# An encoder layer pair on one core: from a scheduler's order to an order fixed by the program

## The chip, the cores and the metric

One core of a Trainium2 chip. The metric is the device time of the whole program in microseconds (us). All arithmetic is float32 in and out; products run on TensorE either as true float32 or as float32r, a faster format into which a float32 number is split in two parts (high and low).

## The reference

Two sequences (2048 and 512 tokens, width 1024) pass through one even and one odd layer with the same weights. Cut to what matters:

```python
# even layer
u = x @ w_in                                  # q,k,v,z of GLA; decay input; q,k,v,z of banded attention
ya = gla_mixer(qa, ka, va, za, gd, ...)       # gated linear attention, forward and backward in time
yb = swa_mixer(qb, kb, vb, zb, rel_bias, sink)# |i-j| <= 128, 8 heads, 2 key/value heads
x = layer_norm(alpha * x + concat([ya, yb]) @ w_out)
# odd layer
bg, cg, h, z = split(x @ w_in, 4)
conv = conv3(cg * h)                          # over time, width 3, per channel
x = layer_norm(alpha * x + (silu(z) * bg * conv) @ w_out)
```

## The kernel before, in words

The 2560 tokens are five groups of 512 (groups 0 to 3 are the long sequence, 4 the short one) and 20 chunks of 128. Intermediate results go through DRAM tensors (`q_s`, `k_s`, `d_s`, `mix_s`, `x1_s` and so on). The work falls into stages.

- **Dense stages.** `e1(g)` projects a group: eight weight tiles moving (`dense_tok`, L207) and 21 blocks with the weights stationary (`dense_ch`, L193). `out_even(g)` is the output projection with residual and layer norm, `odd(g)` the odd layer: 32 blocks (eight times z, c, h, b) and an output projection. Every dense product is three float32r passes: weight high times input high and low (L200, L201), weight low times input high (L204). `weight` (L177) loads a weight tile `ws`, casts it to `wh` on ScalarE, and subtracts on GpSimd to get `wl`; three `ws` and two each of `wh` and `wl` exist.
- **Attention.** `bwd` (L415) runs over the chunks from the last to the first and stores a state for each. `gla` (L450) does one chunk: seven levels of doubling block size, each with DVE products of keys and queries with decays (L520, L525, L527) and a set of small matmuls (L474, L505, L511, L514), then the products with the values and the states (L545, L554). `swa` (L580) does one banded block: scores (L605, L606), bias and maximum (L607), exponential (L616), scaling (L620), transposes (L627), copies (L630, L632) and the value product in true float32 (L635).
- **Order.** The Tile scheduler sets the order on each engine from priorities: matmuls of dense stages in the order of the program text, all that goes through `Urgent` (L97) ahead of the rest; so an instruction of a dense stage's other engines goes first, and attention fills in as the scheduler's own model of time finds it ready. In `run` (L809) `e2_group(g)` is chunk by chunk `gla` and then `swa`; `odd(4)` and `out_even(0)` come after all groups.
- Instructions that go through `Urgent` are all put down to L108; they are told apart by their tiles.

Of the kernel before, what the change touches and what calls it, by code (L numbers as in the profile page):

```python
# [10 lines left out]
F32 = mybir.dt.float32  # L11
# [6 lines left out]
D = 1024  # L18
# [12 lines left out]
def make_layout(i):  # L31
    """Host side: slices, transposes and replicas of the inputs, and arrays that depend on shapes alone."""
# [64 lines left out]
class Urgent:  # L97
    """An engine whose instructions are scheduled ahead of those that are not urgent."""

    def __init__(self, tc, engine):  # L100
        self.tc, self.engine = tc, engine

    def __getattr__(self, name):
        f = getattr(self.engine, name)

        def call(*a, **k):
            with self.tc.high_priority(1000000):
                return f(*a, **k)  # L108
        return call


class Engines:
    def __init__(self, tc, nc, tensor):
        self.tensor = Urgent(tc, nc.tensor) if tensor else nc.tensor
        self.vector, self.scalar, self.gpsimd, self.sync = (
            Urgent(tc, e) for e in (nc.vector, nc.scalar, nc.gpsimd, nc.sync))


class Trunk:
    def __init__(self, tc, nc, I, y_out, ctx):  # L120
        self.tc, self.nc, self.I, self.y_out = tc, nc, I, y_out
        self.dense = Engines(tc, nc, False)
        self.first = Engines(tc, nc, True)
# [6 lines left out]
        self.md = P("mdp", 4)  # L130
        self.mg = P("mgp", 3)
        self.ms = P("msp", 3)
        self.small = P("small", 3)
# [10 lines left out]
        self.qb_s = dr("qb_s", (NC, 64, 8, 128))  # L144
        self.kb_s = dr("kb_s", (64, 2, T))
        self.vb_s = dr("vb_s", (NC, 128, 128))
# [3 lines left out]
        self.up = None  # L150
        self.mix_s = dr("mix_s", (NG, 2, 128, 4, 512))
        self.x1_s = dr("x1_s", (T, D))
        self.sf = {}

    # ---------------------------------------------------------------- helpers
# [12 lines left out]
    def mG(self, shape=(128, 512), dt=F32):  # L168
        return self.mg.tile(list(shape), dt, tag="mg", name="mg")

    def mS(self, shape=(128, 512), dt=F32):
        return self.ms.tile(list(shape), dt, tag="ms", name="ms")
# [4 lines left out]
    def weight(self, src, n=1024):  # L177
        """Load n columns of float32 weights and split them exactly into two float32r parts."""
        nc = self.dense
        raw = self.wp.tile([128, 1024], F32, tag="ws", name="ws", bufs=3)[:, :n]  # L180
        nc.sync.dma_start(raw, src)
        hi = self.wp.tile([128, 1024], F32R, tag="wh", name="wh")[:, :n]
        lo = self.wp.tile([128, 1024], F32R, tag="wl", name="wl")[:, :n]
        nc.scalar.copy(hi, raw)
        nc.gpsimd.tensor_tensor(lo, raw, hi.bitcast(F32), op=ALU.subtract)
        return hi, lo

    def split(self, raw, hi, lo):
        nc = self.dense
        nc.scalar.copy(hi, raw)  # L190
        nc.vector.tensor_tensor(lo, raw, hi.bitcast(F32), op=ALU.subtract)

    def dense_ch(self, src, xh, xl):  # L193
        """[128 channels, 512 tokens] = w^T x, weights stationary."""
        nc = self.dense
        wh, wl = self.weight(src.rearrange("p k c -> p (k c)"))
        p = self.acc.tile([128, 512], F32, tag="acc", name="acc")
        for k in range(8):
            c = slice(k * 128, k * 128 + 128)
            nc.tensor.matmul(p[:], wh[:, c], xh(k), start=(k == 0), stop=False)  # L200
            nc.tensor.matmul(p[:], wh[:, c], xl(k), start=False, stop=False)  # L201
        for k in range(8):
            c = slice(k * 128, k * 128 + 128)
            nc.tensor.matmul(p[:], wl[:, c], xh(k), start=False, stop=(k == 7))  # L204
        return p

    def dense_tok(self, src, n, tiles):  # L207
        """[128 tokens, n columns] per token tile, weights moving. tiles: list of (xh(k), xl(k), pool)."""
        nc = self.dense
        out = []  # L210
        for i, t in enumerate(tiles):
            out.append(self.acc.tile([128, 512], F32, tag="acc", name="acc")[:, :n] if i < 4 else self.pw()[:, :n])
        for kc in range(4):
            wh, wl = self.weight(src[kc].rearrange("p k c -> p (k c)"), 2 * n)
# [11 lines left out]
            for (xh, xl), p in zip(tiles, out):  # L226
                high(xh, xl, p)
                if kc == 3:
                    low(xh, p)
            if kc < 3:  # L230
                for (xh, xl), p in zip(tiles, out):
                    low(xh, p)
        return out

    def log_sig(self, z, out):
        """out = log(sigmoid(z)) = min(z, 0) - log(1 + exp(-|z|))"""
        nc = self.dense
# [5 lines left out]
    def silu(self, z, out, g=None):  # L243
        """out = silu(z) (times g per partition)"""
        nc = self.dense
# [7 lines left out]
    def rstd(self, nc, out, var, scale, eps):  # L253
        nc.scalar.activation(out, var, AF.Ln, scale=scale, bias=eps)
        nc.scalar.activation(out, out, AF.Exp, scale=-0.5)

    # ---------------------------------------------------------------- constants
    def load(self, n, shape, dt=F32):
        t = self.const.tile(list(shape), dt, name=n)
        self.dense.sync.dma_start(t[:], self.I[n])  # L260
        return t

    def setup(self):
        nc, I, c = self.nc, self.I, self.const
# [11 lines left out]
    def setup_up(self):  # L276
        """The up-projections of the decays, split into float32r parts and stacked, with the bias as two rows."""
        nc, I = self.dense, self.I
        self.up = []
        raw = self.e2.tile([128, 4, 512], F32, tag="QK", name="QK")  # L280
        hi = self.e2.tile([128, 2, 512], F32R, tag="Q", name="Q")
        for d, n in enumerate("bf"):
            nc.sync.dma_start(raw[:, d], I["up_" + n])
            lo = raw[:, 2 + d]
# [3 lines left out]
            st = self.e2.tile([128, 512], F32R, tag="ln" + n, name="ln" + n)  # L288
            nc.vector.scalar_tensor_tensor(st[:], hi[:, d].bitcast(F32), self.hl[:, 0:1], lo, op0=ALU.mult, op1=ALU.add)
            self.up.append(st)  # L290

    def setup_late(self):
        nc, I, c = self.nc, self.I, self.const
# [8 lines left out]
    def setup_bias(self):  # L302
        nc, I, c = self.nc, self.I, self.const
        oh = self.mS((32, 512))
        nc.sync.dma_start(oh[:], I["onehot"])
        ml = self.mS((8, 512))
        nc.sync.dma_start(ml[:], I["mline"])
        rb = c.tile([32, 8], F32, name="relb")
        nc.sync.dma_start(rb[:], I["relb"])
        p = self.pw()  # L310
        nc.tensor.matmul(p[:8], rb[:], oh[:], start=True, stop=True)
        line = self.mS((8, 512))
        nc.vector.tensor_tensor(line[:], p[:8], ml[:], op=ALU.add)
        nc.sync.dma_start(self.line_s, line[:])
        for h in range(8):
            rows = self.mS()
            nc.sync.dma_start(rows[:], self.line_s[h:h + 1].broadcast_to([128, 512]))
            nc.sync.dma_start(self.bias_s[h], rows[:])
        self.bias = c.tile([128, 8, 384], F32, name="bias")
        b = self.bias_s  # L320
        nc.sync.dma_start(self.bias[:], bass.AP(b.tensor, b.offset + 127, [[511, 128], [65536, 8], [1, 384]]))

    # ---------------------------------------------------------------- even layer, projections
    def e1(self, g):
        nc, I = self.dense, self.I
        xh, xl = [], []
        for hf in range(2):
            lo = self.stp.tile([128, 4, 512], F32R, tag="st", name="st")
            hi = self.stp.tile([128, 4, 512], F32R, tag="st", name="st")
            for k in range(0, 4, 2):  # L330
                n = 1 if g in (0, 4) else 2
                if g:
                    r = self.yp.tile([128, 2, 512], F32, tag="y", name="y")
                    r = [r[:, 0:1], r[:, 1:2]] if n == 1 else [r[:]]
                else:
                    r = [self.m2((128, 1, 512))[:] for _ in range(2)]
                for i, t in enumerate(r):
                    nc.sync.dma_start(t, I["xT"][g, hf, :, k + i:k + i + n])
                    for j in range(n):
                        self.split(t[:, j], hi[:, k + i + j], lo[:, k + i + j])  # L340
            xh.append(hi)
            xl.append(lo)
        fh = lambda k: xh[k // 4][:, k % 4]
        fl = lambda k: xl[k // 4][:, k % 4]
# [3 lines left out]
        p0 = self.dense_tok(I["w_tok"][0], 336, tiles)  # L348
        for t in range(4):
            v = self.m2()  # L350
            nc.scalar.copy(v[:, :336], p0[t])
            nc.sync.dma_start(self.v_s[4 * g + t, :, :336], v[:, :336])
        p1 = self.dense_tok(I["w_tok"][1], 336, tiles)
        rs = []
        for t in range(4):
            r = self.m2()
            nc.vector.tensor_copy(r[:, :336], p1[t])
            nc.sync.dma_start(self.v_s[4 * g + t, :, 336:], r[:, :176])
            nc.sync.dma_start(self.vb_s[4 * g + t], r[:, 176:304])
            rs.append(r)  # L360
        pg = self.pd()
        for t in range(4):
            nc.tensor.transpose(pg[:32, t * 128:t * 128 + 128], rs[t][:, 304:336], self.ident[:])
        if self.up is None:
            self.setup_up()
        G = self.m2(dt=F32R)
# [489 lines left out]
```

## Time and profile before

| | us |
|---|---|
| median of 3 runs (lowest, highest) | 2750.6 (2750.18, 2762.8) |
| span of the profiled execution | 2753.3 |
| TensorE busy in it (share) | 2582.3 (94%) |
| VectorE (DVE) busy | 1488.7 (54%) |
| ScalarE (ACT) busy | 1201.6 (44%) |
| GpSimd (POOL) busy | 929.6 (34%) |
| DMA: share of the 16 engines, all queues | 49.4% |

The span runs from the first to the last instruction of the profiled execution; no other time of that execution is given. A matmul's row shows how long one takes from start to end; they overlap, so the pace is read from one start to the next. In rows of a timeline the columns are start, length, engine, line, operation, tiles (written<-read), count, and in brackets the idle time ahead with what ended it. In rows of stretches they are the stretch, its length, the busy time of each engine with its instructions, and then the granted clock of TensorE and the DMA's share.

### The profile page before, as it was taken

The numbers are of one execution on the slowest core, as the hardware profiler recorded it, in microseconds if no ns is written. First come the engines' busy times: TensorE is split into PE (matmuls) and PEld (weight loads), VectorE is DVE, ScalarE is ACT, GpSimd is POOL, SyncE is SP. The second block draws the span as 40 slices with busy tenths as digits, with TensorE's granted clock in tenths as the row PEclk, the third lists the DMA queues.
The fourth block names the chain that finished last, engine by engine and source line by source line (L and its number), as shares of the span: only waits on it lengthen the run. The fifth ranks groups of instructions, "written<-read, shape, count | busy, mean of one in ns | idle before, by whom it ended". The sixth has DMA issues, their size and how long they took to land.

```text
span 2753.3 us, 41852 instructions
## 1 busy us (share of the span) xinstructions
PE 2582.3 (94%) x16214; PEld 2034.7 (74%) x16214; DVE 1488.7 (54%) x2595; ACT 1201.6 (44%) x2246; POOL 929.6 (34%) x409
## 2 busy tenths in 40 slices
PE   8999999899999989999988889989999999999998
PEld 7887876687778866666665666668788878878887
DVE  3222377632252277787778877863553455345335
ACT  5545555345435545444443344443334423432431
POOL 3433322233434412212222222224444434434442
PEclk9999999999999999999999999999999999999999
DMA  7667554557458644343445464423652355234322
GB/s 251 192 204 227 157 168 138 171 178 220 148 169 263 187 144 124 101 139 110 142 131 189 153 196 134 126 77 103 209 176 93 134 176 180 92 123 156 112 96 88
DMA packets 258549, 425.19 MB, mean 154 GB/s; under 512 B 38656, under 2 KB 152064, under 8 KB 258352
## 3 DMA queue, kind: packets, MB, share of 16 engines
q1 hardware_dynamic: 258352, 422.53, 49.0%
q8 instruction: 128, 2.10, 0.3%
q14 instruction: 69, 0.57, 0.1%
HBM read 339.59 MB, written 82.85 MB: 153 GB/s over the span
## 4 chain that ended last, share of the span: by engine, by line
PE 39%; DVE 6%; issue 2%; DMA 2%; ACT 1%; SPq 0%; DVEq 0%; ACTq 0%
PE acc L201 8%; PE acc L200 8%; PE acc L204 8%; PE acc L224 3%; PE acc L220 3%; PE acc L219 3%; PE pss L635 1%; DVE y L108 1%; PE pss L627 1%; PE psg L545 1%; DMA md<-mix_s 1%; DVE QK L525 1%; DMA md<-x_s 1%; DMA P<-kb_s 0%; PE psg L474 0%
## 5 line engine op out<-in xcount | busy, mean ns | idle before, releaser
L108 POOL TENSOR_TENSOR wl<-ws,wh 128x1024 fp32r<-128x1024 f32 (+1 forms) x381 | 902.3, 2369 | 1679.4 <-PE acc L204 829.4
L200 PE MATMUL acc<-st,wh 128*128 128x512 f32 x2120 | 844.0, 398 | 0.0
L201 PE MATMUL acc<-st,wh 128*128 128x512 f32 x2120 | 842.7, 397 | 0.0
L108 ACT CAST wh<-ws 128x1024 fp32r<-128x1024 f32 (+1 forms) x381 | 388.0, 1018 | 586.3 <-PE acc L201 214.6
L204 PE MATMUL acc<-st,wl 128*128 128x512 f32 x2120 | 547.2, 395 | 0.0
L200 PEld LDWEIGHTS acc<-st,wh 128*128 128x128 f32 x2120 | 404.1, 191 | 81.8 <-issue 2.6
L201 PEld LDWEIGHTS acc<-st,wh 128*128 128x128 f32 x2120 | 404.1, 191 | 80.2 <-issue 0.4
L204 PEld LDWEIGHTS acc<-st,wl 128*128 128x128 f32 x2120 | 396.0, 188 | 82.5 <-issue 3.0
L219 PE MATMUL acc<-wh,st 128*128 128x512 f32 (+1 forms) x872 | 324.4, 375 | 20.2 <-ACT st L108 13.3
L220 PE MATMUL acc<-wh,st 128*128 128x512 f32 (+1 forms) x872 | 322.3, 372 | 0.0
L108 ACT ACTIVATE md<-md 128x512 f32<-128x512 f32 x360 | 227.6, 632 | 123.4 <-DVE md L108 116.1
L108 DVE SCALAR_TENSOR_TENSOR md<-acc,md 128x512 f32<-128x512 f32 x120 | 82.7, 689 | 357.8 <-ACT md L108 354.9
L224 PE MATMUL acc<-wl,st 128*128 128x512 f32 (+1 forms) x872 | 220.3, 371 | 0.0
L219 PEld LDWEIGHTS acc<-wh,st 128*128 128x128 f32 x872 | 167.1, 192 | 47.0 <-ACT st L108 13.7
L220 PEld LDWEIGHTS acc<-wh,st 128*128 128x128 f32 x872 | 167.3, 192 | 21.5 <-DVE st L108 0.2
L224 PEld LDWEIGHTS acc<-wl,st 128*128 128x128 f32 x872 | 157.0, 191 | 24.2 <-issue 3.4
L108 ACT ACTIVATE md<-acc 128x512 f32<-128x512 f32 x160 | 93.7, 597 | 73.5 <-PE acc L204 67.7
L635 PE MATMUL pss<-ms,V 128*64 128x512 f32 x224 | 119.4, 622 | 6.2 <-DVE ms L632 6.0
L108 DVE TENSOR_TENSOR md<-md,acc 128x512 f32<-128x512 f32 x40 | 27.5, 687 | 179.8 <-PE acc L204 179.8
L108 ACT CAST st<-md 128x512 fp32r<-128x512 f32 x88 | 53.5, 620 | 159.1 <-DVE md L108 131.3
L627 PEld LDWEIGHTS pss<-ident,P 128*128 128x128 f32 x448 | 56.5, 145 | 88.7 <-DVE P L620 44.5
L627 PE MATMUL pss<-ident,P 128*128 128x128 f32 x448 | 92.2, 292 | 31.4 <-DVE P L620 31.4
(170 smaller groups left out, 2987.1 us busy)
## 6 DMA issues: line engine op xcount, KB each, us to landing
ws<-in_w_od SPq DMA_DIRECT2D x160, 512.0 KB, 3.5
ws<-in_w_ch SPq DMA_DIRECT2D x105, 512.0 KB, 3.7
ws<-in_w_oe SPq DMA_DIRECT2D x40, 512.0 KB, 3.6
ws<-in_w_oo SPq DMA_DIRECT2D x40, 512.0 KB, 3.5
ws<-in_w_tok SPq DMA_DIRECT2D x40, 336.0 KB, 2.9
d_s<-md SPq DMA_DIRECT2D x40, 256.0 KB, 3.1
tA<-d_s SPq DMA_DIRECT2D x20, 512.0 KB, 4.6
P<-qb_s SPq DMA_DIRECT2D x40, 256.0 KB, 4.6
```

Source lines behind the costliest of these rows:

```text
L108: return f(*a, **k)
L200: nc.tensor.matmul(p[:], wh[:, c], xh(k), start=(k == 0), stop=False)
L201: nc.tensor.matmul(p[:], wh[:, c], xl(k), start=False, stop=False)
L204: nc.tensor.matmul(p[:], wl[:, c], xh(k), start=False, stop=(k == 7))
L219: nc.tensor.matmul(p, xh(k), wh[:, c], start=(k == 0), stop=False)
L220: nc.tensor.matmul(p, xl(k), wh[:, c], start=False, stop=False)
L224: nc.tensor.matmul(p, xh(k), wl[:, c], start=False, stop=(k == 7))
L525: nc.vector.tensor_tensor(qq, qq, tot(1, n - 1), op=ALU.mult)
L545: nc.tensor.matmul(po[:, h], l, r, start=(i == 0), stop=(i == len(mm) - 1))
L627: nc.tensor.transpose(pt[:, gq], Pt[:, 4 * kv + gq, kb * 128:kb * 128 + 128], self.ident[:])
L635: nc.tensor.matmul(po[64 * kv:64 * kv + 64], V[:, kb, 64 * kv:64 * kv + 64], PT[kv][:], start=(kb == 0), stop=(kb == nk - 1), tile_positio ...
```

## The change

The scheduler is switched off (`manual_schedule`), and the program text is the order of each engine. The text is produced by a small planner, `Flow`: dense stages are one generator, all else is "side" generators. A generator yields after each piece with numbers of its own: TensorE time, a wait until its next piece may follow, and DVE time. The planner adds these up in a clock of its own and, at each yield of the dense generator (in a weight-stationary block: after 8 matmuls, after 16, and behind its evacuation), emits the side pieces whose time has come. Where a dense stage needs something that is not there yet, `until` emits side pieces alone until it is.

```diff
+    def pump(self):
+        self.flush()
+        for s in sorted(self.side, key=lambda s: s[0]):
+            if s[0] <= self.t:
+                self.step(s)
...
+    def until(self, key):
+        while key not in self.done:
+            ready = [s for s in self.side if s[3] is None or s[3] in self.done]
...
+            self.t = max(self.t, s[0])
+            self.flush()
+            self.step(s)
...
+    def weight(self):
+        if not self.cooked:
+            self.cook()
+        w = self.cooked.pop(0)
+        self.cook()
+        return w
...
-        self.e1(3)
-        self.bwd_seq(4)
-        self.e2_group(4)
...
-        for g in range(4):
-            self.e2_group(g)
-        self.odd(4)
-        self.out_even(0)
...
+        stages = [("e1", 4), ("e1", 3), ("e1", 2), ("e1", 1), ("e1", 0), ("oe", 4), ("odd", 4), ("oe", 0),
+                  ("oe", 1), ("odd", 0), ("oe", 2), ("odd", 1), ("oe", 3), ("odd", 2), ("odd", 3)]
...
+        flow.add(self.gla_stream())
+        flow.add(self.swa_stream())
```

- `gla_stream` goes through the backward states of group 4, the chunks 16 to 19, the backward states of groups 3 to 0, then the chunks 0 to 15. `swa_stream` is a second stream of its own: blocks 16 to 19, 13 to 15, 9 to 12, 5 to 8, 0 to 4, each batch once its projection is done. Before, a chunk and its block went together, all 16 of the long sequence behind the projections.
- `cook` emits the cast and the subtraction for the next weight tile when a dense block begins, behind the evacuation of the block before.
- `out_even(4)` stands behind `e1(0)` and right ahead of `odd(4)`, which reads its result through DRAM.
- In `swa` the queries, keys and values are split into high and low when they are projected and stored so (no casts in the block), a block is done in two halves of four heads, and the value product is two float32r passes with 128 columns instead of one float32 product with 64:

```diff
-                nc.tensor.matmul(po[64 * kv:64 * kv + 64], V[:, kb, 64 * kv:64 * kv + 64], PT[kv][:],
-                                 start=(kb == 0), stop=(kb == nk - 1), tile_position=(0, 64 * kv))
...
+                    nc.scalar.copy(ph[:], flat)
+                    nc.vector.tensor_tensor(pl[:], flat, ph[:].bitcast(F32), op=ALU.subtract)
...
+                    nc.tensor.matmul(po[:], vv, old[0][:], start=(kb == 1), stop=False)
+                    nc.tensor.matmul(po[:], vv, old[1][:], start=False, stop=(kb == nk))
...
+            nc.scalar.copy(op[mine], po[other])
+            nc.vector.tensor_tensor(op[mine], po[mine], op[mine], op=ALU.add)
```

- In `gla` the keys are loaded twice instead of copied, and one copy per level (`km`) takes the place of two. The layer norms of a dense stage become side pieces too.

**First place: a level of a chunk among the blocks of `odd(4)`, on TensorE.** Before (`acc` rows are dense, `psg` the chunk, `pss` the banded block; the number behind a tile is its buffer):

```order
L474 MATMUL psg_8623<-QK_8565,mg_8620 32x32 [waits DVE_49,Activation_49]
L474 MATMUL psg_8623<-QK_8565,mg_8620 32x32 x15
L635 MATMUL pss_8528<-ms_8541,V_8469 64x512 [waits DVE_49]
L627 MATMUL pss_8545<-ident_92,P_8457 128x128 [waits PE_49]
L627 MATMUL pss_8545<-ident_92,P_8457 128x128 x3
L201 MATMUL acc_14094<-st_13942,wh_14090 128x512
L204 MATMUL acc_14094<-st_13939,wl_14091 128x512 [waits Pool_49]
L204 MATMUL acc_14094<-st_13939,wl_14091 128x512 x3
L204 MATMUL acc_14094<-st_13940,wl_14091 128x512 x4
L627 MATMUL pss_8552<-ident_92,P_8457 128x128 [waits PE_49,Activation_49]
```

And of the change, in the same stage:

```order
L289 MATMUL acc_10234<-st_9985,wh_10130 128x512
L716 MATMUL psg_10251<-QQ_10091,km_10216 32x32 [waits DVE_49,Activation_49]
L716 MATMUL psg_10251<-QQ_10091,km_10216 32x32 x15
L900 MATMUL pss_10276<-K0_9659,Q_9657 128x384 [waits DVE_49]
L901 MATMUL pss_10276<-K1_9660,Q_9657 128x384
L900 MATMUL pss_10280<-K0_9659,Q_9657 128x384 [waits DVE_49]
L901 MATMUL pss_10280<-K1_9660,Q_9657 128x384
L295 MATMUL acc_10234<-st_9822,wl_10131 128x512 [waits Pool_49]
L295 MATMUL acc_10234<-st_9822,wl_10131 128x512 x3
L295 MATMUL acc_10234<-st_9984,wl_10131 128x512 x4
L288 MATMUL acc_10300<-st_9822,wh_10228 128x512 [waits Activation_49]
```

Attention stood between single dense matmuls, and a dense run of one to nine; now whole pieces stand between runs of 8 or more dense matmuls. TensorE changes between dense work and other work 974 times in the order before and 626 times in the new one.

**Second place: the end of `odd(4)` and the start of `out_even(0)`, on TensorE.** Before, dense follows on dense (`acc_15298` is the last product of `odd(4)`, `acc_15511` the first of `out_even(0)`):

```order
L220 MATMUL acc_15298<-wh_15391,st_14018 128x512
L224 MATMUL acc_15298<-wl_15392,st_14016 128x512 x2
L219 MATMUL acc_15511<-wh_15517,st_15463 128x512 [waits DVE_49,Activation_49]
L220 MATMUL acc_15511<-wh_15517,st_15464 128x512
L219 MATMUL acc_15511<-wh_15517,st_15463 128x512
```

Of the change, behind the last product of `odd(4)` (`acc_12925`):

```order
L315 MATMUL acc_12925<-wl_13060,st_10127 128x512 x2
L829 MATMUL psg_13198<-ident_88,km_13135 128x128 x4
L900 MATMUL pss_13204<-K0_12942,Q_12940 128x384 [waits DVE_49]
L901 MATMUL pss_13204<-K1_12943,Q_12940 128x384
L900 MATMUL pss_13208<-K0_12942,Q_12940 128x384 [waits DVE_49]
L901 MATMUL pss_13208<-K1_12943,Q_12940 128x384
L716 MATMUL psg_13229<-qn_13036,KK_13101 32x32 [waits DMAHW4_49,DMAHW0_49]
L716 MATMUL psg_13229<-qn_13036,KK_13101 32x32 x15
L716 MATMUL psg_13260<-QQ_13224,KK_13101 32x32 [waits DVE_49,PE_49]
```

906 attention matmuls stand here with no dense one between them: five chunks' worth of levels (chunks 6 to 10) and seven halves of banded blocks (blocks 0 to 3 with a half done already, `out_even(0)` needs them all). In the same stretch DVE has 351 instructions. A second, smaller place of the kind stands between `out_even(4)` and `odd(4)`: 260 matmuls on TensorE, 108 instructions on DVE, four layer norms among them.

**Third place: the cast of a weight tile behind SiLU, on ScalarE, in an odd layer.** Before, z is `acc_21577`, and the next blocks use `wh_21611`, `wh_21642`, `wh_21682`:

```order
L108 CAST wh_21642<-ws_21640 128x1024 [waits DMAHW1_49,PE_49,Pool_49]
L108 ACTIVATE mv_21467<-mv_21467,eps_98 128x1 [waits DVE_49]
L108 ACTIVATE mv_21467<-mv_21467 128x1 [waits Activation_49]
L108 ACTIVATE md_21602<-acc_21577 128x512 [waits DMAHW2_49,PE_49]
L108 ACTIVATE md_21602<-md_21602 128x512 [waits Activation_49]
```

Of the change, z is `acc_21116`, and the next blocks use `wh_21110`, `wh_21148`, `wh_21181`:

```order
L263 CAST wh_21110<-ws_21076 128x1024 [waits DMAHW6_49,PE_49,Pool_49]
L332 ACTIVATE md_21141<-acc_21116 128x512 [waits PE_49]
L333 ACTIVATE md_21141<-md_21141 128x512 [waits Activation_49]
L334 ACTIVATE md_21141<-md_21141 128x512 [waits Activation_49]
L341 ACTIVATE md_21141<-md_21141 128x512 [waits DVE_49]
L263 CAST wh_21148<-ws_21114 128x1024 [waits DMAHW7_49,Pool_49]
```

The tile for the second block behind z was cast ahead of the SiLU; now it is cast behind its last step, which waits for DVE, while the block ahead of it runs.

More of the change, by code (lines that the diff above doesn't have):

```diff
@@ new lines, in bwd, with bwd_group @@
+        yield 0.9, 1.5, 1.4
+        return Sn
+    def bwd_group(self, g):
+        c0, c1 = self.seq(g)
+        if 4 * g + 4 == c1:
+            self.bst = None
+        cs = [c for c in range(4 * g + 3, 4 * g - 1, -1) if c > c0]
+        ld = self.bwd_load(cs[0])
+        yield 0.0, 4.0, 0.0
+        for i, c in enumerate(cs):
+            it = self.bwd(c, ld, self.bst)
+            n = 0
+            while True:
+                try:
+                    said = next(it)
+                except StopIteration as s:
+                    self.bst = s.value
+                    break
+                n += 1
+                if n == 3 and i + 1 < len(cs):
+                    ld = self.bwd_load(cs[i + 1])
+                    said = (said[0], max(said[1], 4.0), said[2])
+                yield said
+        if 4 * g == c0:
+            yield 0.0, 8.0, 0.0
@@ L534, in gla @@
             nc.vector.copy_predicated(A[r, :, r], m, acmp[r])
-        Sf = self.sf.get("s") if not first else None
+        ahead(0)
+        yield 0.6, 3.5, 3.4
+        Sf = self.sf if not first else None
+        if not last:
+            pt = self.pg((128, 4, 128))
+            for h in range(4):
+                nc.tensor.transpose(pt[:, h], K[:, 0, h * 128:h * 128 + 128], self.ident[:])
+            kt = self.e((128, 4, 128), "km", bufs=2)
+            nc.scalar.copy(kt[:], pt[:])
         po = self.pg((128, 4, 128))
```

943 lines of the change are left out of this document (595 added, 348 removed).

## The prediction

> **What bounds the kernel now.** I read the busy times first, then how fast TensorE goes where nothing disturbs it, then stretches of the span, and last the waits and single lines within the stretch that is not dense. The page's busy times:
>
> ```profile
> PE 2582.3 (94%) x16214; PEld 2034.7 (74%) x16214; DVE 1488.7 (54%) x2595; ACT 1201.6 (44%) x2246; POOL 929.6 (34%) x409
> ```
>
> TensorE is the bound: idle for 2753.3 − 2582.3 = 171.0 us, while no other engine is busy much over half. How dense is busy? TensorE's timeline late in the span, where only dense blocks are left:
>
> ```profile
> 2403.78 1.98 PE L204 MATMUL acc<-st,wl 128*128 128x512 f32 x8
> 2405.59 0.39 PE L200 MATMUL acc<-st,wh 128*128 128x512 f32 x1
> ...
> 2409.22 1.98 PE L204 MATMUL acc<-st,wl 128*128 128x512 f32 x8
> ```
>
> The 24 matmuls of a block start 2409.22 − 2403.78 = 5.44 us apart: 0.227 us a matmul. Stretches (columns: stretch, length, busy time of PE, PEld, DVE, ACT, POOL, granted clock, DMA share, GB/s):
>
> ```profile
> 0.00:9.00 9.00, 0.13 (x1) 0.13 (x1) 1.00 (x6) 3.27 (x4) 1.80 (x5) 1.00 0.62 174
> 1000.00:1400.00 400.00, 372.38 (x3501) 260.32 (x3500) 317.06 (x629) 187.13 (x460) 88.07 (x41) 0.98 0.43 129
> 1400.00:1870.00 470.00, 416.42 (x3318) 296.54 (x3317) 359.17 (x655) 190.36 (x467) 111.89 (x49) 0.96 0.45 140
> 2290.00:2745.00 455.00, 453.00 (x2007) 374.46 (x2005) 212.14 (x281) 160.84 (x222) 192.31 (x79) 1.00 0.37 121
> 2745.00:2753.00 8.00, 0.38 (x2) 0.00 (x0) 4.16 (x5) 0.50 (x2) 0.00 (x0) 0.74 0.32 131
> ```
>
> The last 455 us are full (2 us idle), so nothing is to be had there. The loss lies where attention runs: 28 + 54 us idle between 1000 and 1870, with DVE busy for 79% and 76% of it. About 9 us at the start and 8 at the end are nobody's to save, which leaves 171 − 17 = 154 us of idle time inside. What it looks like, on TensorE's timeline:
>
> ```profile
> 1302.35 0.46 PE L474 MATMUL psg<-QK,mg 128*32 128x32 f32 x32 [1.99 <-ACT mg L493]
> ...
> 1305.13 0.63 PE L200 MATMUL acc<-st,wh 128*128 128x512 f32 x1
> 1305.56 0.63 PE L201 MATMUL acc<-st,wh 128*128 128x512 f32 x1
> ...
> 1317.93 0.50 PE L201 MATMUL acc<-st,wh 128*128 128x512 f32 x1
> 1318.27 0.40 PE L200 MATMUL acc<-st,wh 128*128 128x512 f32 x1
> ```
>
> and in the largest row of TensorE's waits:
>
> ```profile
> PE pss L627 <- DVE P L620: 31.4, 19, 5.3
> ```
>
> TensorE takes up an attention matmul whose input is not ready and stands, with dense work queued behind it. And busy time hides a second loss: behind small matmuls a dense one starts after 0.34 us (1317.93 to 1318.27) instead of 0.227, and after a pause of 2 us at a pace of 0.43.
>
> **The change part by part.** The sum starts at the span, 2753.3 us; the median of the three runs, 2750.6, lies 0.1% below it, and I make no correction for that.
>
> *The value product.* In the stretch 1000 to 1870, and a pair on the timeline:
>
> ```profile
> L635 PE MATMUL pss<-ms,V 128*64 128x512 f32 x184 | 97.7, 618 | 6.2 <-DVE ms L632 6.0 <-ACT ms L630 0.2
> ```
> ```profile
> 1314.78 1.07 PE L635 MATMUL pss<-ms,V 128*64 128x512 f32 x2
> 1315.78 0.31 PE L474 MATMUL psg<-QK,mg 128*32 128x32 f32 x10
> ```
>
> Two take 1315.78 − 1314.78 = 1.00 us. With the page's count,
>
> ```profile
> L635 PE MATMUL pss<-ms,V 128*64 128x512 f32 x224 | 119.4, 622 | 6.2 <-DVE ms L632 6.0 <-ACT ms L630 0.2
> ```
>
> 112 pairs are 112 us. A pair becomes two passes for each of its two halves of key columns in all heads, 224 passes at the dense pace, 50.8 us: −61. The two evacuations behind a half (a copy on ScalarE, an add on DVE) are hidden, if dense work is there.
>
> *Fewer changes of work.* 974 − 626 = 348 of them go. One costs 0.34 − 0.227 = 0.11 us if the next matmul waits for it, nothing if it is hidden: 0 to 38; I take the middle, −20.
>
> *The old waits.* All 154 us go: each was tied to an order that is no longer there. What comes in their place is costed below.
>
> *New: two stretches with no dense work.* Behind `out_even(4)`, four layer norms, a store and loads of the result, and transposes have to be done before `odd(4)` starts; and `out_even(0)` waits for the banded blocks 0 to 3, which come late in their stream. There DVE's chain sets the time. Its mean instruction in the stretches above takes (317.06 + 359.17) / (629 + 655) = 0.527 us. The DMAs:
>
> ```profile
> x_s<-y SPq DMA_DIRECT2D x20, 512.0 KB, 3.6
> ...
> md<-x_s SPq DMA_DIRECT2D x40, 256.0 KB, 4.0
> ```
>
> The first stretch: 108 × 0.527 = 57, and 3.6 + 4.0 for the way through DRAM, 65 us. TensorE's own work in it is not lost. By tile, in 1000 to 1870 (`psg` above, `pss` below), and the number of chunks:
>
> ```profile
> 1000.00:1870.00 870.00, 151.41 (x4181) 122.19 (x4181) 49.26 (x147) 50.90 (x210) 0.97 0.44 135
> ```
> ```profile
> 1000.00:1870.00 870.00, 233.07 (x792) 105.24 (x792) 105.56 (x182) 26.90 (x46) 0.97 0.44 135
> ```
> ```profile
> L545 PE MATMUL psg<-mg x120: 275/275/422, 1029.4 to 1833.2; 128*128 128x128 f32 x120
> ```
>
> 120 at 8 a chunk are 15 chunks, so 151.41 / 15 = 10.1 us a chunk. 184 of 224 value products are 16.4 of 20 blocks: 233.07 / 16.4 = 14.2 each; 97.7 / 16.4 = 6.0 of it goes and 50.8 / 20 = 2.5 comes: 10.7 a block, 5.4 a half. The first stretch holds one chunk, two and a half halves and some transposes, 10.1 + 13.5 + 4 = 28: +37 of idle time. The second: 351 × 0.527 = 185, less 5 × 10.1 + 7 × 5.4 = 88: +97. Its bounds: in it no weight is split, so GpSimd is quiet. On the timeline at 2400, with GpSimd subtracting:
>
> ```profile
> 2400.45 2.41 POOL L108 TENSOR_TENSOR wl<-ws,wh 128x1024 fp32r<-128x1024 f32 x1 [2.76 <-PE acc L204]
> 2401.26 2.14 DVE L108 TENSOR_TENSOR md<-md 128x512 f32<-128x512 f32 x1
> ...
> 2404.02 1.05 ACT L108 CAST wh<-ws 128x1024 fp32r<-128x1024 f32 x1
> 2404.09 0.69 DVE L108 TENSOR_TENSOR st<-md,st 128x512 fp32r<-128x512 f32 x1 [0.69 <-ACT st L108]
> ```
>
> A DVE product takes 2.14 us there, and 0.69 without. The chunks' large products, in 1000 to 1870:
>
> ```profile
> L525 DVE TENSOR_TENSOR QK<-QK,tA 128x512 f32<-128x512 f32 x80 | 76.1, 951 | 16.9 <-PE psg L505 16.8
> ```
>
> If the some 70 instructions of this kind drop from 0.951 to 0.69, the stretch is 18 us shorter: +79. If DVE, its chain broken by the other engines, is busy for only (317.06 + 359.17) / 870 = 78% as above, it is 185 / 0.78 = 238 long: +150. I take +97, since a chunk and a banded block can fill each other's gaps. The Trainium skill, "GPSIMD Engine Reference", section 1, says that GpSimd shares its SBUF interfaces with VectorE and contends with its instructions that have two SBUF inputs. The two rows above agree, and by that rule the lower price, +79, would hold and the sum be 18 us less.
>
> *New waits.* A whole piece is now put between runs of 8 or more dense matmuls, by the planner's numbers. Where its input is late, TensorE stands and all dense work behind it. The bounds are nothing and as much as before (154); a run of 8 is 1.8 us of cover, against the 2.0 us wait in the row at 1302.35, so most is covered: a quarter, +38. Second, each weight tile's cast now stands behind the evacuation chain of a block, on ScalarE. With SiLU:
>
> ```profile
> 2405.79 0.60 ACT L108 ACTIVATE md<-acc 128x512 f32<-128x512 f32 x1 [0.71 <-PE acc L204]
> 2406.42 1.30 ACT L108 ACTIVATE md<-md 128x512 f32<-128x512 f32 x2
> 2408.47 0.63 ACT L108 ACTIVATE md<-md 128x512 f32<-128x512 f32 x1 [0.76 <-DVE md L108]
> ```
>
> The block ends at 2405.59, the chain at 2409.10, a cast of 1.05 behind it at 2410.15: 4.56 of the 5.44 us until the tile is needed. The 0.88 us left is spent once the last step waits 2.14 us for a DVE product, or DVE is busy with attention; behind the cast wait GpSimd's subtraction and then TensorE. There are 16 such chains in each of five projections and 8 in each of five odd layers, 120; 72 of them (two projections, the odd layers) stand among attention. At a third of a us: +24.
>
> *Edits that I cost at nothing.* Splitting queries and keys once, at their projection, takes the block's casts away and puts them under dense blocks; the second load of the keys in place of copies, the single copy per level, and a few products moved to GpSimd are off TensorE, with DMA at 0.45 and GpSimd at 112 of 470 us in the stretch above; DVE's total stays about even. SP's stores now come some pieces behind their data; later readers are a stage away, but for `out_even(4)`, which is in the sum.
>
> The sum: 2753.3 − 61 − 20 − 154 + 37 + 97 + 38 + 24 = 2714.
>
> **The rivals.**
>
> *The weave is clean.* The new waits (38 + 24) are nothing, since the planner adds DVE's time up too: 2714 − 62 = 2652. For it speaks the stretch 2290 to 2745, where all of SiLU is hidden under dense blocks; against it, the 78% of DVE.
>
> *The waits only change places.* The planner's clock drifts from the chip's, and half of the old waits come back: 77 + 24 in place of 62, 2714 + 39 = 2753, no change. For it: one attention product on DVE takes 0.69 to 2.14 us, depending on GpSimd; a fixed order cannot give way, while one late piece makes the next ones late. Against: the pieces have spare runs between them.
>
> *Late weights: slower.* The price is a us for each of the 120 chains instead of 24 in all: 2714 + 96 = 2810. The place is the second block behind SiLU or a decay, and it decides when ScalarE's last Exp waits over 0.88 us longer than in the rows above. It turns slower than before at (2764 − 2690) / 120 = 0.62 us each. For it: one conflict with GpSimd adds 2.14 − 0.69 = 1.45; the planner puts attention pieces' copies ahead of the cast too. Against: in most odd layers little attention is left, and two blocks of four have no such chain.
>
> *A slow clock in the empty stretches.* In the rows above the granted clock is 0.96 to 0.98 with idle time and 1.00 without, and after 2 us of pause dense matmuls came at 0.43, half pace. If TensorE stays at half pace in both empty stretches, the six chunks' matmuls there, in the chain with DVE, take twice as long: 6 × 10.1 = 61, giving 2775. The Trainium skill, "TensorE: Matmul & The Clock Gate", section "What's actually happening", has the clock halved after an idle window of about 3.4 us, and released by a busy one. Against it: the matmuls of a level are not far apart, so whole empty windows may be rare.
>
> **How the numbers follow.** About 0.5%, 13.8 us, is what a measurement of this kernel can tell from no change: faster is below 2737, slower above 2764. The forecast (2690 to 2737) has 0.42, the clean weave 0.16, together faster 0.58. The waits that change places have 0.20, which is same. Late weights 0.15 and the slow clock 0.07 make slower 0.22. The range goes from the clean weave with the cheap second stretch and all changes of work counted, 2652 − 18 − 18 = 2616, to late weights, 2810; I give 2620 to 2810.
>
> **What would show it.** In the new profile: the value product's rows sum to about 51 us; TensorE stands for about 37 us ahead of `odd(4)` and for 80 to 150 ahead of `out_even(0)`, both with DVE busy for most of it; `wh` as the cause of idle time ahead of dense blocks is about 24 us; waits of attention matmuls between dense runs about 38. I am wrong if the empty stretches cost TensorE under 60 us or over 200, if dense blocks wait for weights for over 75 us, or if the idle time within the woven stages stays above 100 us.

## The result, and the profile after

The changed kernel takes 2897.4 us (median of 4 runs, 2895.79 to 2898.91) against 2756.7 for the kernel before on the same chip: ratio 1.0515, 95% interval 1.0485 to 1.0546. It is slower by 5%, where 1.3% faster was forecast. The page's busy times:

```profile
span 2896.8 us, 41921 instructions
...
PE 2565.4 (89%) x16214; PEld 2095.6 (72%) x16214; DVE 1573.7 (54%) x2770; ACT 1195.4 (41%) x2240; POOL 968.8 (33%) x409
```

TensorE is busy for 17 us less and idle for 331.4 instead of 171.0. Stretches, cut where the dense stream stops:

```profile
0.00:1073.70 1073.70, 965.51 (x5578) 809.73 (x5579) 518.16 (x1044) 555.58 (x1034) 358.82 (x169) 0.97 0.61 191
1073.70:1138.30 64.60, 36.36 (x414) 26.55 (x413) 53.50 (x110) 24.18 (x67) 1.27 (x1) 0.72 0.49 164
1138.30:1466.30 328.00, 306.03 (x2500) 246.08 (x2499) 227.18 (x391) 136.59 (x286) 108.29 (x44) 0.96 0.40 134
1466.30:1652.90 186.60, 118.54 (x1589) 87.66 (x1587) 148.29 (x351) 69.50 (x201) 4.45 (x3) 0.65 0.38 124
1652.90:2881.00 1228.10, 1138.35 (x6139) 925.42 (x6138) 615.78 (x864) 408.52 (x650) 495.92 (x192) 0.97 0.40 135
```

The second and fourth are the two stretches without dense work: 64.6 and 186.6 us long, forecast as 65 and 185. (The profile has two rows for most matmuls of a chunk, so the 906 of the order are 1589 in the fourth row, three dense ones among them.) Idle in them are 28 + 68 us. The other 235 lie outside: 16 at the start, 15 at the end, and 108.2 − 15.9 + 22.0 + 89.8 = 204 where dense work is there, for which the forecast had 62; over 100 there was one of its own signs of being wrong. TensorE's waits of dense matmuls (`acc`), the first five and the last of eleven rows:

```profile
PE acc L310 <- DVE y L1021: 39.1, 7, 15.7
PE acc L310 <- ACT wh L263: 22.1, 5, 15.9
PE acc L288 <- ACT wh L263: 17.3, 16, 2.5
PE acc L288 <- DVE md L534: 14.6, 4, 5.3
PE acc L310 <- DVE md L343: 12.3, 4, 4.5
...
PE acc L289 <- DVE st L495: 0.4, 2, 0.2
```

The eleven sum to 124.9 us, of which 15.9 is the start. Before, nine such rows sum to 30.5:

```profile
PE acc L219 <- ACT st L108: 13.3, 2, 8.9
...
PE acc L108 <- DVE y L108: 0.4, 1, 0.4
```

So 109 of the 204 are the dense stream waiting for steps of its own stages, and 95 are attention's. The two largest rows of attention (`psg`, here with the empty stretches counted in):

```profile
PE psg L716 <- ACT km L775: 30.0, 15, 5.9
PE psg L749 <- DVE QQ L763: 26.6, 21, 2.9
```

The longest dense wait behind the start, in `out_even(1)` behind the second empty stretch, on SyncE's queue and then on DVE:

```profile
1744.08 11.24 SPq L990 DMA_DIRECT2D x_s<-y  x2
1755.37 1.26 SPq L476 DMA_DIRECT2D md<-x_s  x2
...
1757.66 2.79 SPq L1013 DMA_DIRECT2D y<-in_x  x4
```
```profile
1751.80 3.17 DVE L987 SCALAR_TENSOR_TENSOR y<-y,mv,lnb 128x1024 f32<-128x1024 f32 x1
...
1765.85 0.69 DVE L1021 SCALAR_TENSOR_TENSOR y<-y,acc 128x512 f32<-128x512 f32 x1 [9.59 <-DMA y<-in_x]
```

The norm's stores stand in the queue for 11.24 us until DVE, in turn with attention's products, has ended the norm at 1755; the residual loads stand behind them; the sum that frees an accumulator comes at 1765.85, and TensorE's next dense matmul waits 15.7 us for it.

### The profile page after: what moved, and what is told of

Same layout as the page of the kernel before. It is cut to its first block, busy times and chain, and to the rows that moved or that the text cites. A ratio compares the mean times of both kernels' runs of the same rounds, so it can differ in the third digit from the quotient of the medians.

```text
span 2896.8 us, 41921 instructions
## 1 busy us (share of the span) xinstructions
PE 2565.4 (89%) x16214; PEld 2095.6 (72%) x16214; DVE 1573.7 (54%) x2770; ACT 1195.4 (41%) x2240; POOL 968.8 (33%) x409
## 5 line engine op out<-in xcount | busy, mean ns | idle before, releaser
L264 POOL TENSOR_TENSOR wl<-ws,wh 128x1024 fp32r<-128x1024 f32 (+1 forms) x381 | 930.2, 2442 | 1682.5 <-ACT wh L263 1455.5
L288 PE MATMUL acc<-st,wh 128*128 128x512 f32 x2120 | 847.8, 400 | 35.7 <-ACT wh L263 17.3
L295 PE MATMUL acc<-st,wl 128*128 128x512 f32 x2120 | 535.5, 395 | 0.0
L310 PE MATMUL acc<-wh,st 128*128 128x512 f32 (+1 forms) x880 | 337.4, 385 | 79.2 <-DVE y L1021 39.1
L311 PE MATMUL acc<-wh,st 128*128 128x512 f32 (+1 forms) x880 | 328.6, 375 | 0.0
L310 PEld LDWEIGHTS acc<-wh,st 128*128 128x128 f32 x880 | 173.9, 198 | 109.7 <-DVE y L1021 25.4
L311 PEld LDWEIGHTS acc<-wh,st 128*128 128x128 f32 x880 | 173.8, 198 | 22.2
L934 DVE TENSOR_TENSOR ptl<-pss,pth 128x512 fp32r<-128x512 f32 x112 | 77.1, 688 | 120.9 <-ACT pth L933 120.3
L278 DVE TENSOR_TENSOR st<-md,st 128x512 fp32r<-128x512 f32 x80 | 92.1, 1157 | 78.1 <-ACT st L277 73.4
L332 ACT ACTIVATE md<-acc 128x512 f32<-128x512 f32 x120 | 71.5, 596 | 143.4 <-PE acc L295 133.7
L775 ACT COPY km<-KK 128x512 f32<-128x512 f32 x80 | 50.9, 636 | 162.9 <-DVE KK L758 146.6
L915 ACT ACTIVATE P<-P,nm 128x384 f32<-128x384 f32 (+1 forms) x160 | 93.1, 583 | 58.3 <-DVE nm L910 58.3
L929 PE MATMUL pss<-ident,P 128*128 128x128 f32 x448 | 86.1, 313 | 23.9 <-DVE P L921 19.4
```

The lines of the kernel that those rows point to most:

```text
L310: nc.tensor.matmul(p, xh(k), wh[:, c], start=(k == 0), stop=False)
L311: nc.tensor.matmul(p, xl(k), wh[:, c], start=False, stop=False)
L915: nc.scalar.activation(Pt[:, h, :w], Pt[:, h, :w], AF.Exp, bias=nm[:, h:h + 1], accum_out=den[:, h:h + 1])
L929: nc.tensor.transpose(pt[:, gq], Pt[:, gq, kb * 128:kb * 128 + 128], self.ident[:])
```

## The experiments

Times are medians; unless said, differences are to the changed kernel's 2897.4.

**Where the attention stands.** Four kernels shift attention against dense work. First, the order of the banded stream:

```diff
-(2, range(9, 13)), (1, range(5, 9)), (0, range(5))]
+(2, range(9, 13)), (0, range(5)), (1, range(5, 9))]
```

> Only the order of the banded stream is changed: blocks 0 to 4 ahead of 5 to 8. Theory (the loss is where the dense stream runs out, since the banded blocks come late): out_even(0) no longer waits for the last blocks, out_even(0) and out_even(1) give some 88 us of dense work under the attention that stood alone, and the 116 us lost ahead of out_even(0) shrink by 60 to 90: 2810 to 2840 us. odd(0) still needs all blocks, so a rest of the stretch moves ahead of it. Rival (the loss is VectorE's conflict with GpSimd and waits all over): the place of the stretch doesn't matter, 2885 to 2900.

2863.5 (−34), between the two. The second stretch is 141 us instead of 187, with another of 28 ahead of it.

```diff
-            if k == 3:
-                yield 8 * MM, 0.0
...
+            if k % 2:
+                yield 4 * MM, 0.0
...
```

> A weight-stationary block lets the planner in after every 8 matmuls... of a pass pair after every 4 instead of 8, and in the middle of its last pass, so that side pieces get twice the places. Theory (a banded block takes 72 us, since each of its some 18 pieces waits for the next stop of the dense stream, though the planner's own waits add up to about 44): blocks take 55 to 62 us, the stretch ahead of out_even(0) loses most of its 116 us, 2780 to 2830 us in all. Rival (the planner's waits are too short for the chip, so pieces come before their inputs): denser pieces stand more, 2890 to 2950.

2888.4 (−9), far from the theory: the stretch ahead of `out_even(0)` falls to 98 us, the other rises to 74, and TensorE's idle time stays at 2885.4 − 2556.6 = 329 us.

```diff
-("e1", 1), ("e1", 0), ("oe", 4), ("odd", 4)
+("e1", 1), ("oe", 4), ("e1", 0), ("odd", 4)
```

> out_even(4) goes ahead of e1(0) instead of behind it (the decay weights are reloaded in e1(0) from DRAM, since the layer norm's constants share their tile). Theory: the 65 us stretch ahead of odd(4) goes, with its 42 us lost: 2845 to 2865 us. Rival (the attention that ran there comes back in the next stretch without dense work): 2885 to 2900.

2883.7 (−14): the first stretch is gone, the second is 226 us. The rival is nearer: the stretch moved.

```diff
-        s[0] = max(self.t + wait, ...)
+        s[0] = max(self.t + 0.5 * wait, ...)
```

> The planner counts half of each side piece's wait, so that attention goes in faster while dense work is there. Theory (the weave is too thin: between 1138 and 1466 DVE is busy for 69% only, and the attention left over then stands alone): the stretches ahead of odd(4) and out_even(0) lose 60 to 120 of the 158 us they cost, waits in the weave grow by less, 2800 to 2860 us. Rival (the waits are what the chip needs): TensorE stands as much more in the weave as the stretches shrink, 2880 to 2930.

2906.7 (+9): the stretches are 78 and 72 us, 101 less, and all of it comes back as waits in the weave. The rival holds. With these four, that the thin weave is the loss has fallen for the greater part: attention that is moved is paid for elsewhere, but for 9 to 34 us in three of them.

**What the conflict and the clock cost.** In the changed kernel and in the one before, GpSimd's subtraction is left out:

```diff
+            lo = self.low[:, :n]
...
-            nc.gpsimd.tensor_tensor(lo, raw, hi.bitcast(F32), op=ALU.subtract)
```

> GpSimd's subtraction is left out: all weight tiles use one constant low part, so the products leave out the weights' low parts; ScalarE's cast stays. Theory: only the woven stretches gain, some 218 us idle there of which a quarter to a third is VectorE held up; stretches without dense work stay as they are: 2830 to 2860 us. Rival (all new waits are this conflict): 2700 to 2760.

> The kernel before with one constant low part for all weight tiles in place of GpSimd's subtraction, so that its products leave out the weights' low parts. In the changed kernel the same edit gave 109 us. If the conflict costs only a fixed order so much: 2690 to 2730 us, 20 to 60 gained; if it costs both alike: 2640 to 2660.

2788.3 (−109, between its two ranges) and 2618.5 against 2756.8 (−138, below both of its own). The stretches without dense work stay at 66 and 186 us. The busy times of `before_quiet`:

```profile
PE 2558.1 (98%) x16214; PEld 2012.9 (77%) x16214; DVE 1234.2 (47%) x2595; ACT 1205.9 (46%) x2246; POOL 27.4 (1%) x29
```

The same 2595 instructions keep DVE busy for 1234.2 instead of 1488.7 us, and TensorE is idle for 59.0 instead of 171.0. (The constant low part is zero, and the granted clock is 0.994 instead of 0.981; TensorE's busy time is 24 us less. Whether the zeros have a part in these 24 is not shown.) The conflict is large, but it costs the kernel before as much: without it the changed kernel is still 170 us behind, so it is not what the change lost.

```diff
+            if self.warm and key[:1] == "o":
+                self.warm()      # three dense matmuls, result unread
             self.step(s)
```

> Where only side pieces are emitted ahead of an out_even or odd stage, three dense matmuls whose result nobody reads are put ahead of each piece, to hold the granted clock up. Theory (62 us of the 158 lost in the two stretches are matmuls at a lower clock, half of them in the chain): granted clock there from 0.65 and 0.72 to over 0.9, 2850 to 2880 us. Rival (the stretches are VectorE's chain alone): 2890 to 2930, since the added matmuls stand in the way.

2909.7 (+12), in the rival's range. A row from inside the second stretch, and the added matmuls in it:

```profile
1480.00:1666.60 186.60, 169.87 (x1887) 130.51 (x1887) 142.25 (x335) 70.75 (x205) 4.51 (x3) 0.98 0.37 120
```
```profile
L1181 PE MATMUL acc<-wl 128*128 128x512 f32 x373 | 109.8, 416 | 0.0
```

The granted clock is 0.98 instead of 0.65, and the stretches are 74 and 197 us long, 10 longer each: as a remedy it does not pay. What the slow clock costs by itself it does not show, since the added matmuls now fill TensorE, busy for 170 of 187 us. A bound comes from the changed kernel: DVE is busy for 148 of the 187 us of the second stretch, so with DVE's work as it is no clock could shorten it by more than 38 us; the rows in which DVE waits directly for TensorE there sum to 12.

**Mending single edges in the fixed order.** `early` emits the next tile's cast behind the 16 matmuls that read `wh`:

```diff
+        self.early()
         yield 8 * MM, 0.0
         for k in range(8):
             nc.tensor.matmul(p[:], wl[:, c], xh(k), ...)
```

> In a weight-stationary block the cast of the next tile is emitted behind the 16 matmuls that read the tile's high parts, ahead of the block's evacuation, SiLU and the side pieces there; GpSimd's subtraction stays where it was. Theory (dense waits for wh are 39 us in all, and some 9 of the stretches' neighbours): 2865 to 2885 us. Rival (late weights were the cause of my forecast's miss): 2800 or less. If ScalarE is merely busy: 2890 to 2900.

2868.2 (−29), in the theory's range, but only in part by its mechanism: the dense waits for `wh` and `wl` fall by 8 us, from 42.8 to 34.8, of 24 that TensorE's idle time falls by.

```diff
-            self.flow.add(self.norms(ys, rows, gb, dst, key))
+            for _, _, d in self.norms(ys, rows, gb, dst, key):
+                self.flow.dve = max(self.flow.dve, self.flow.t) + d
```

> The four layer norms of an output projection are emitted at once behind its last evacuation, instead of as side pieces among the attention. Theory (dense matmuls wait 125 us for work of their own stages that now stands in line behind attention pieces, 39 us of them for the residual sums, which wait for y buffers that the norms hold): waits behind y sums fall from 39 to under 15 us, 2860 to 2880 us. Rival (these waits lie beside the attention's own chain, which sets the end of the stretch): 2890 to 2905.

2940.4 (+43), worse than either theory. The waits behind `y` fall from 39.1 to 8.4 us, as the theory had it; new ones stand in their place:

```profile
PE acc L310 <- ACT wh L263: 37.3, 5, 14.9
PE acc L288 <- ACT st L494: 27.3, 2, 13.7
...
PE pss L489 <- DVE st L495: 17.3, 1, 17.3
```

The norm's square root on ScalarE now stands, waiting for DVE, ahead of casts and splits that do not need it; four such waits, 3.6 to 4.6 us each, come ahead of this split:

```profile
2136.54 0.29 ACT L349 ACTIVATE mv<-mv,eps 128x1 f32<-128x1 f32 x1 [3.62 <-DVE mv L983]
...
2136.98 0.57 ACT L494 CAST st<-pss 128x512 fp32r<-128x512 f32 x1
```

On DVE the four norms stand ahead of attention in the same way: one `psg` matmul waits 20.1 us behind them. `edges_first` also takes the `yield` out of the loop of evacuations:

> As norms_first, and the four evacuations of a projection's second half are emitted at once, with no side piece between. Theory: the 15 us that dense blocks wait for the last evacuation go too, 10 to 15 us below norms_first. Rival: attention stands behind them instead, the same time within 5 us.

2937.5 (+40): 3 below `norms_first`, the rival. All of these with `cast_early` and `swa_low_first`, and then only the last two:

> norms_first, edges_first, cast_early and swa_low_first in one. Theory (separate losses, so the gains add up: 20 to 35 for the first two, 29, 34): 2790 to 2820 us, still above the kernel before, since most of the stretch without dense work is left. Rival (they are one loss that moves): 2840 to 2870.

> cast_early and swa_low_first in one, the order fixed by the program. If the two are separate: 29 + 34 off, 2830 to 2840 us. If they are one loss that moves: 2850 to 2870.

2897.8 (0, worse than either range) and 2846.0 (−51, between the two). The gains of two add up to 51 of 63; the norms take all of it away again. Last, residual loads sooner and splits closer, with `cast_early`'s edit:

```diff
-        self.flow.add(residuals(), 12.0)
+        self.flow.add(residuals(), 0.0)
...
-            yield 0.0, 2.5, 0.8
+            yield 0.0, 1.0, 0.8
```

> Fixed order, with cast_early's edit, residual loads 12 us sooner by the planner's clock, and the pieces that split a stage's input 1.0 instead of 2.5 us apart. If moving these few ahead by hand is what the scheduler gains: 2780 to 2830 us. If the gain lies in the fine order of all engines: 2850 to 2870, cast_early's gain and little else.

2877.2 (−20), 9 worse than the cast alone: moving these few groups by hand is not what pays.

**Giving the order back.** The changed kernel's text, with the scheduler on; in the second kernel with the old priorities as well:

```diff
-            with tc.manual_schedule():
-                trunk.run()
+            trunk.run()
```

> The changed kernel's text with the scheduler switched on again, with the text as its order of priority: the same work, the same stages and streams, but an instruction may go ahead of one that is not ready by the scheduler's model. TensorE's longest stretches without dense work hold 729 and 224 attention matmuls instead of 906 and 260. Theory (the loss is the fixed order): 2760 to 2830 us, the waits of dense matmuls well under 125 us. Rival (the work and the stage order): 2870 or more.

> As scheduler_order, and with the priorities of the kernel before: all but the dense matmuls goes ahead of them. No stretch without dense work is left that holds over 150 matmuls, and TensorE changes between dense and other work 1064 times. Theory (the new banded attention is worth its 57 us of TensorE once the order is the old kind): 2680 to 2730 us. Rival (the text's streams and gates cost it): 2760 or more.

2638.6 (−259, 121 below the theory's range; ratio to before 0.9585, 0.9538 to 0.9631) and 2719.4 (in the theory's range; ratio 0.9879, 0.9846 to 0.9912). The first has the same instructions and nearly the same number of changes of work on TensorE (672 against 626). Its busy times, its stretches but for the last 8 us, and the first and the last of its 13 rows of dense waits:

```profile
PE 2494.7 (95%) x16214; PEld 2059.5 (78%) x16214; DVE 1574.2 (60%) x2770; ACT 1204.5 (46%) x2240; POOL 946.1 (36%) x409
```
```profile
0.00:972.00 972.00, 935.67 (x5577) 794.59 (x5578) 525.27 (x1055) 554.54 (x1036) 363.97 (x169) 0.99 0.70 214
972.00:1022.00 50.00, 35.05 (x364) 26.10 (x363) 45.26 (x91) 20.15 (x49) 3.65 (x2) 0.62 0.74 245
1022.00:1346.00 324.00, 316.71 (x2747) 255.00 (x2746) 259.77 (x449) 152.04 (x326) 107.98 (x45) 0.99 0.45 144
1346.00:1480.00 134.00, 87.17 (x1274) 66.49 (x1273) 110.45 (x269) 53.90 (x161) 6.99 (x4) 0.75 0.50 159
1480.00:2626.00 1146.00, 1120.11 (x6259) 917.32 (x6257) 629.28 (x904) 423.37 (x667) 463.55 (x189) 0.99 0.42 141
```
```profile
PE acc L310 <- ACT st L277: 7.6, 1, 7.6
...
PE acc L288 <- DVE tB L765: 0.7, 1, 0.7
```

Dense waits are 35.7 us instead of 124.9, 7.6 of them the start; the stretches without dense work are still there, 50 and 134 us, with 15 + 47 us of idle time. Where dense work is there TensorE is idle for 36.3 − 7.6 + 7.3 + 25.9 = 62 us, 142 less than in the fixed order. In all, idle time falls by 192 us (331.4 to 139.2) and busy time by 71 (2565.4 to 2494.7). Matched row by row in the traces, the scheduler moves SyncE's residual loads `y<-in_x` ahead by 101 places on the mean, DVE's input splits by 23, ScalarE's casts by 3.6, and a dense token block's matmuls by 28; DVE's residual sums stay within 3 places. This settles the cause: the loss is the order that the planner's pieces give each engine, not the work, the streams or the stage order. (Both orders are static; the scheduler sets its own instruction by instruction on each engine, the planner by whole pieces on all of them at once.)

**A version faster than both.** `weight` computes a tile's low part once and stores it; the four later uses load it:

```diff
-        nc.gpsimd.tensor_tensor(lo, raw, hi.bitcast(F32), op=ALU.subtract)
...
+        if kept is None:
+            nc.gpsimd.tensor_tensor(lo, raw, hi.bitcast(F32), op=ALU.subtract)
...
+            nc.sync.dma_start(kept, lo.bitcast(F32))
+        else:
+            nc.sync.dma_start(lo.bitcast(F32), kept)
```

> The kernel before, in which a weight tile's low part is computed by GpSimd only the first time and stored to DRAM; the four later uses load it. GpSimd's subtractions fall from 381 to about 77, and 304 loads of up to 512 KB are added. If the conflict with VectorE is what held attention up (138 us with all subtractions gone) and the DMA has room at half load: 2640 to 2680 us. Rival (the added DMA makes weight tiles late): 2740 or more.

> scheduler_urgent with low_kept's edit: GpSimd computes a weight tile's low part once, later uses load it. If the gains of both add up: 65 us below scheduler_urgent, 2610 to 2670 us. If the added loads stand in the way of the added loads of keys: no more than 20 below it.

> scheduler_order with low_kept's edit (GpSimd computes each low part once, later uses load it). If the gains add up (66 for the kernel before, 52 with scheduler_urgent): 2570 to 2595 us. If the two stretches without dense work, where GpSimd is quiet anyway, hold most of the rest: 2600 to 2620.

In the kernel before 2686.5 (6 above its range; ratio 0.9763, 0.9735 to 0.9791), with `scheduler_urgent` 2667.3 (0.9689, 0.9653 to 0.9725), with `scheduler_order` 2627.0 (0.9542, 0.9521 to 0.9563). The gain falls from 66 to 52 to 12 us, where the intervals with and without it overlap; its rival (2600 to 2620) was nearer. The text in the scheduler's hands is the version that beats both.

## Why the prediction was wrong

- **What bounds the kernel** was right: TensorE, by what it waits for.
- **The value product** (−61) was sized too large. Counted in the traces from each start to the next, at most a matmul's own length, it is 112 us before, 74 in the changed kernel and 69 in `scheduler_order`: −38 and −44. A pass came every 0.31 us on the median, not at the dense pace of 0.227. Its rows in the changed kernel run from start to end and overlap with other matmuls, so their sum, 106.8 us, cannot be held against the 51 that I had named as a sign:

```profile
L939 PE MATMUL pss<-pth,V 128*128 128x512 f32 x112 | 58.0, 518 | 16.7 <-DVE ptl L934 9.9 <-ACT pth L933 6.6
L940 PE MATMUL pss<-ptl,V 128*128 128x512 f32 x112 | 48.8, 436 | 1.3 <-DVE ptl L934 1.3
```

- **Fewer changes of work** (−20): counted the same way, all dense matmuls together sum to 2099.9 us before, 2098.0 in the changed kernel and 2056.0 in `scheduler_order`. In the fixed order next to nothing of it came.
- **The two stretches** were right in place. That their lengths came so close (64.6 and 186.6 us for 65 and 185) is luck: in the second the mean DVE instruction took 148.29 / 351 = 0.42 us where I took 0.527, and DVE was busy for 79% of it where I took all; the two misses cancel. The price in idle time is 96 us instead of 134, because TensorE is busy for 155 us there, where I took 28 + 88 of work; the granted clock is 0.72 and 0.65.
- **The old waits** (−154) **and the new** (+38, +24): the new waits are the step that failed. For 62 us, 204 came. Attention's are 95 instead of 38: "a run of 8 is 1.8 us of cover" was the fault, since a run covers only a wait that ends within it, and the planner put pieces in front of TensorE whose inputs from DVE and ScalarE were not there. For dense work only late weights were priced, and their rows came to the size (22.1 − 15.9 + 17.3 + 3.4 = 27 us for 24), though `cast_early` took only 8 us off them. Not priced at all were the dense stages' other steps, 109 − 27 = 82 us: residual sums, evacuations and input splits, which now stand in line behind attention. I had SP's late stores as free but for `out_even(4)`; the rows at 1744 show one that is not. That the old waits go with the old order was not the fault by itself: `scheduler_order` loses 62 us where dense work is there, as much as I had for the new waits, with the same pieces and GpSimd's subtractions in place. What I had not seen is that an order of whole pieces, the same on all engines, cannot keep the new waits so small. Many of the old ones hang on GpSimd's conflict with DVE, as `before_quiet` shows (59 us of idle time instead of 171).
- The account of the 183 us between forecast and span: 142 are these waits (204 − 62); 64 are busy time of TensorE (23 of the value product, 18 of changes of work, 23 of other attention matmuls); 14 are start and end (31 instead of 17); the idle time of the stretches is 38 less.
- **Rivals.** "The waits only change places" named the mechanism, but with half the size. Late weights at 1 us each did not come. The slow clock came (0.65 and 0.72), but no run shows what it costs alone. The Trainium skill, "TensorE: Matmul & The Clock Gate", section "What's actually happening", lets the clock fall after idle windows: the rows agree that it falls where TensorE stands, and its price here is not shown. The Trainium skill, "GPSIMD Engine Reference", section 1, says that GpSimd shares its interfaces to SBUF with VectorE: the lower price that I had from it for the second stretch agrees with the trace (a product `KK<-KK,tB` of a chunk took 0.675 us there and 0.928 over the whole kernel). What the conflict costs the whole kernel, 109 and 138 us by `quiet_pool` and `before_quiet`, I had not priced.
- **Open:** which of the scheduler's moves carries most of the 259 us. `cast_early` gained 29 in the fixed order; residual loads and splits moved by hand gave nothing more.

## What to carry to other kernels

Before an order is written by hand, sum what each in-order engine and each DMA queue holds up behind an instruction that waits, the dense stream's own evacuations, loads and splits first: here they cost 82 us that no term had. A good text is worth having as the scheduler's priority: the same text was 5% slower than before as an order and 4% faster as a priority. Attention that was moved away from one empty stretch came back for the most part as another stretch or as waits: of four tries the best gained 34 us.

## What the hardware showed unexpectedly

GpSimd's two-input subtraction, which no wait of TensorE in the kernel before names, costs 138 us of 2757: without it DVE is busy for 254 us less with the same instructions. Matmuls added to hold the granted clock at 0.98 instead of 0.65 made a stretch of small matmuls 10 us longer. In the kernel before, loading the low parts raises the DMA's mean from 154 to 230 GB/s, at no loss that shows:

```profile
DMA packets 313414, 617.77 MB, mean 230 GB/s; under 512 B 44752, under 2 KB 158160, under 8 KB 313216
```
